# Second block's mixer: the value projection ahead of the SSM outputs, the attention outputs ahead of the gate, w_out from the attention half on

## The chip, the cores and the metric

The program runs on one core of a Trainium2 chip, in one launch. The metric is the device time of one execution in microseconds (us), taken as the median of several executions. Beside it stands one profiled execution, whose trace gives every instruction of every engine: TensorE (PE: matmuls; PEld: its weight loads), VectorE (DVE), ScalarE (ACT), GpSimd (POOL) and SyncE (SP, which here only issues DMAs).

## The reference

A sequence of 256 tokens of width 1024 goes through four transformer layers (attention of three kinds, each followed by a SwiGLU feed-forward net), all in 32-bit floats. Then comes one hybrid layer, "the second block". Its mixer, cut to what matters:

```
h = rmsnorm(x) ; u, q, k, v = split(h @ w_in)            # four parts of 512 columns
y_ssm  = gelu(C * scan(A, B u) + d * u)                  # state-space branch (SSM), from u
y_ssm  = y_ssm * sigmoid(y_ssm @ w_glu + b_glu)          # its gate
y_attn = softmax(causal(q k^T / 8)) v                    # 8 heads of 64, all 256 keys
mix = concat(rmsnorm(y_ssm) * g_ssm_out, rmsnorm(y_attn) * g_attn_out)
x = x + rmsnorm(mix @ w_out) * g_post_mix                # then a SwiGLU net closes the layer
```

The two branches meet only in `mix`: rows 0 to 511 of `w_out` multiply the SSM branch, rows 512 to 1023 the attention branch.

## The kernel before

The 256 tokens are two tiles of 128 (t = 0, 1). A weight matrix is streamed in units of 512 KB (two blocks of 128 rows by 512 columns, or one shape of the same size). `wload` (lines 155 to 159) fetches a unit into `raw` through SyncE's queue, ScalarE rounds it to `hi` (L158) and VectorE takes the rest as `lo` (L159); `mm3` (L178, L179, L180) then makes three products of 512 columns for each block of 128 rows: one unit costs 6 products for each token tile. There are 4 buffers for `raw` and 6 each for `hi` and `lo`. `proj` runs such a projection and hands the finished sums, which lie in PSUM, to a consumer; `outacc` adds a piece of an output projection into four PSUM banks.

PSUM has 8 banks: four named `acc`, two `E`, two `T`. Scratch tiles come from `work`, whose buffers are shared by size: tiles of more than 512 floats a partition have three buffers in all, those of 257 to 512 floats eight. In the mixer the large kind holds, among others, `ut` (the turned SSM input), two `xp` (the SSM states), `vs` (the values), `yo` and `ys` (the SSM outputs before and after their way back to token order).

The order of the program text is not the order in which an engine works: a planner gives each engine a fixed order ahead of the run, from its own estimate of when each instruction can go. Among those that can go it takes the one that stands first in the text. So what stands later in the text fills gaps that the planner sees. Each engine then runs its order strictly, and waits where something is late.

`mixer2` (from line 1128 on) has in its text:

1. the projection of u, the turning of u by small DMAs, the inflow products (L1174) and the scan on VectorE, which leaves `xp`;
2. the projections of q and k (after each one a fetch of a table pair `kd`, `vd` for the SSM outputs: L1124, L1125), turned by `to_T`;
3. the scores (L1225) for each t and each parity e of the head, and for each group the softmax numerators: masked maximum on VectorE (L541, L544), exponentials on ScalarE (L546), transposes (`transp`, L280) and a copy to `aTs` (L528, L530);
4. the SSM outputs: for each half b, 32 products with `ut` and 64 with `xp` (all at L252, the line of the helper `Chain`), in one `acc` bank; then the GELU (L1253 to L1259) into `yo`, and eight DMAs (L1262) that carry `yo` into `ys`;
5. the projection of v, 4 units and 48 products, in two `acc` banks, which `consu` (L1139) copies to `vs`;
6. the turning of `ys` to `yT` (L280, L272, L273) and the gate's projection with `w_glu`, in the two `E` banks, with its consumer `consg`; the gated result goes through `normed` (L1274 to L1277), which turns it into blocks 0 to 3 of `mT`;
7. the attention outputs: 16 products for t = 0 and 32 for t = 1 (L252 again, with `aTs` and `vs`), scaled, and through `normed` into blocks 4 to 7 of `mT`;
8. `w_out` rows 0 to 511 (SSM), then rows 512 to 1023 (attention), the last with the consumer that closes the layer's first part.

`normed` leaves its four transposes in a list; `pump`, called after each unit's products, takes one such entry off the list. The tail of the text that the change touches:

```
        proj(yT, [(I["w_glu_2"][0], 0, 512)], consg, tmaj=True, tags=("EE",))
        for t in range(NT):
            po, pm = psum("TE"[t]), Chain()
            ...
            normed(ya, 1.0, rows[0], t, slice(4, 8))
        outacc(acc, mT, 0, wo, 0, 4, True, False)
        ...
        outacc(acc, mT, 4, wo, 4, 4, False, True, consume)
```

Of the kernel before, what the change touches and what calls it, by code (L numbers as in the profile page):

```python
# [9 lines left out]
F32R = mybir.dt.float32r  # L10
AF = mybir.ActivationFunctionType
ALU = mybir.AluOpType
AX = mybir.AxisListType

S = 256
D = 1024
NT = 2
# [49 lines left out]
def tile_kernel(ctx, tc, I, out, upto=99):  # L67
    nc = tc.nc
    V, A, T, G = nc.vector, nc.scalar, nc.tensor, nc.gpsimd
    ids = [0]  # L70

    def nm(s):
        ids[0] += 1
        return f"{s}_{ids[0]}"
# [13 lines left out]
    def psum(tag):  # L88
        return pp.tile([128, 512], F32, tag=tag, name=nm("ps" + tag), bufs=BANKS[tag])

    def big(shape, dt=F32):
        return bp.tile(shape, dt, tag="big", name=nm("big"))

    def work(shape, tag, dt=F32):
        n = int(np.prod(shape[1:]))
        tg, b = ("w05", 4) if n <= 128 else ("w1", 3) if n <= 256 else ("w2", 8) if n <= 512 else ("w4", 3)
        if tag == "aT":
            tg = "aT"
        return wk.tile(shape, dt, tag=tg, name=nm(tag), bufs=b)
# [5 lines left out]
    def cs(t):  # L105
        return slice(t * 128, (t + 1) * 128)
# [40 lines left out]
    def row(ap, width):  # L147
        g = work([128, width], "gb")
        nc.sync.dma_start(g, ap.partition_broadcast(128))
        return g  # L150
# [13 lines left out]
    def pump(n=1):  # L164

        for _ in range(min(n, len(waiting))):
            waiting.pop(0)()
# [14 lines left out]
    def proj(xT, specs, consume, tmaj=False, kx=0, tags=(), mid=None):  # L182

        def units(spec):
            w, c0, n = spec
            nk = w.shape[0] // 128
            ku = 1024 // n if n <= 256 else 2
            for k in range(0, nk, ku):
                m = min(ku, nk - k)
                yield k, m, nk, w[k * 128:(k + m) * 128, c0:c0 + n], n  # L190

        if tmaj and len(specs) > 1 and sum(sp_[2] for sp_ in specs) > 512:
            proj(xT, specs[:1], consume, True, kx, tags[:1], mid)
            proj(xT, specs[1:], lambda i, t, p_: consume(i + 1, t, p_), False, kx, tags[1:])
        elif tmaj:
            us = []
            for sp_ in specs:
                us.append([])
                for k, m, nk, ap, n in units(sp_):
                    us[-1].append((k, nk, n, wload(ap, m, n)))  # L200
                    if mid and k == 0:
                        mid()
            for t in range(NT):
                for i, u in enumerate(us):
                    p_ = psum(tags[i][t] if i < len(tags) else "acc")
                    for k, nk, n, un in u:
                        mm3(p_[:, :n], xT, t, kx + k, un, n, k == 0, k + un[0].shape[1] == nk)
                        pump()
                    consume(i, t, p_[:, :n])
        else:  # L210
            for i, sp_ in enumerate(specs):
                p_ = [psum(tags[i][t] if i < len(tags) else "acc") for t in range(NT)]
                for k, m, nk, ap, n in units(sp_):
                    un = wload(ap, m, n)
                    for t in range(NT):
                        mm3(p_[t][:, :n], xT, t, kx + k, un, n, k == 0, k + m == nk)
                    pump()
                for t in range(NT):
                    consume(i, t, p_[t][:, :n])
# [38 lines left out]
    def newacc():  # L258
        return [[None, None] for _ in range(NT)]
# [6 lines left out]
    def split_out(dst, blocks, t, pt, scale=None):  # L266

        n = blocks.stop - blocks.start
        src = pt[:, :n * 128].rearrange("p (c q) -> p c q", c=n)
        hi, lo = dst[0][:, blocks, cs(t)], dst[1][:, blocks, cs(t)]  # L270
        if scale is None:
            A.activation(hi, src, AF.Copy)  # L272
            V.tensor_tensor(lo, src, hi.bitcast(F32), op=ALU.subtract)  # L273
        else:
            A.activation(hi, src, AF.Copy, scale=scale)
            V.scalar_tensor_tensor(lo, src, scale, hi.bitcast(F32), op0=ALU.mult, op1=ALU.subtract)

    def transp(pt, i, src):
        n = src.shape[1]
        T.transpose(pt[:n, i * 128:(i + 1) * 128], src, ident)  # L280
# [6 lines left out]
    def pair():  # L287
        return big([128, KC, S], F32R), big([128, KC, S], F32R)
# [839 lines left out]
    def mixer2(P, close):  # L1128
        hT, r = P.hT, P.r
        wt, (e_, i_, d_) = TAB["in"]  # L1130
        w = I["w_in_2"][0]
# [3 lines left out]
        tt = lambda o, a, b, op: V.tensor_tensor(o, a, b, op=op)  # L1135

        def consu(c, t, p_):
            if c == 3:
                A.activation(vs[:, t], p_, AF.Copy, scale=r[:, t:t + 1])  # L1139
                return  # L1140
            dst = work([128, 512], "qs")
            A.activation(dst, p_, AF.Copy, scale=r[:, t:t + 1])
            if c == 0:

                for q_ in range(4):
                    (G if q_ == 3 else nc.sync).dma_start(uc[32 * q_ + 16 * t:32 * q_ + 16 * t + 16], dst[:, cs(q_)])
            else:
                to_T(qkT, 4 * (c - 1), dst, 4, t, (A, V)[c - 1])
# [68 lines left out]
        for t in range(NT):  # L1217
            k = 128 * (t + 1)
            s8 = sums[t] = small(16, "s8")
            for e in range(2):  # L1220
                for pr in prs[t]:
# [5 lines left out]
                    p_ = work([128, n, k], "p2")  # L1227
                    st = small(4, "st")
                    heads(E, n, k, 0.125, st[:, 0:n], s8[:, 4 * e + pr[0]:4 * e + pr[0] + n], p_, caus[:, t, 0:k])
                    aTs[t, e, pr] = tr4([p_[:, a, cs(c)] for a in range(n) for c in range(t + 1)], (A, V)[e])  # L1230

        yb = [psum("acc"), psum("acc")]
        yo = work([128, 8, 8, 16], "yo")
        ys = work([128, NT, 512], "ys")
# [26 lines left out]
            for q_ in range(4):  # L1261
                nc.sync.dma_start(ys[:, t, cs(q_)], yo[32 * q_ + 16 * t:32 * q_ + 16 * t + 16].rearrange("c i g h -> c i (g h)"))  # L1262

        proj(hT, [(w, 1536, 512)], lambda c, t, p_: consu(3, t, p_))

        mT = pair()
        rows = [row(I[n_][0], 512) for n_ in ("g_attn_out_2", "b_glu_2", "g_ssm_out_2")]
        G.tensor_scalar(rows[2], rows[2], 0.5, None, op0=ALU.mult)

        def normed(src, half, grow, t, blocks):  # L1270

            st = small(2, "stn")
            j = work([128, 512], "junk")
            A.activation(j, src, AF.Square, scale=half * 512 ** -0.5, accum_out=st[:, 0:1])  # L1274
            rsq(st[:, 1:2], st[:, 0:1])
            o = work([128, 512], "nrm")
            V.scalar_tensor_tensor(o, src, st[:, 1:2], grow, op0=ALU.mult, op1=ALU.mult)  # L1277

            def turn():
                pt = psum("T")  # L1280
                for c in range(4):
                    transp(pt, c, o[:, cs(c)])
                split_out(mT, blocks, t, pt)

            waiting.append(turn)


        yT = (big([128, 4, S], F32R), big([128, 4, S], F32R))
        for t in range(NT):
            pt = psum("T")  # L1290
            for c in range(4):
                transp(pt, c, ys[:, t, cs(c)])
            split_out(yT, slice(0, 4), t, pt)

        def consg(c, t, p_):
            z = work([128, 512], "zg")
            tt(z, p_, rows[1], ALU.add)
            A.activation(z, z, AF.Tanh, scale=0.5)
            V.scalar_tensor_tensor(ys[:, t], z, 1.0, ys[:, t], op0=ALU.add, op1=ALU.mult)
            normed(ys[:, t], 0.5, rows[2], t, slice(0, 4))  # L1300

        proj(yT, [(I["w_glu_2"][0], 0, 512)], consg, tmaj=True, tags=("EE",))
        for t in range(NT):
            po, pm = psum("TE"[t]), Chain()
            s8 = sums[t]
            for e in range(2):
                for pr in prs[t]:
                    for a, d in enumerate(pr):
                        h = 2 * d + e
                        for c in range(t + 1):  # L1310
                            pm(po[:, 64 * h:64 * h + 64], aTs[t, e, pr][:, (t + 1) * a + c], vs[:, c, 64 * h:64 * h + 64],
                               start=(c == 0), stop=(c == t))
            pump()
            V.reciprocal(s8[:, 8:16], s8[:, 0:8])
            ya = work([128, 512], "ya")
            d4 = lambda z: z.rearrange("p (d e v) -> p d e v", d=4, e=2)
            for e in range(2):
                V.tensor_tensor(d4(ya)[:, :, e], d4(po)[:, :, e], s8[:, 8 + 4 * e:12 + 4 * e].unsqueeze(2).to_broadcast([128, 4, 64]),
                                op=ALU.mult)
            normed(ya, 1.0, rows[0], t, slice(4, 8))  # L1320
        wo = I["w_out_2"][0]
        acc = newacc()
        outacc(acc, mT, 0, wo, 0, 4, True, False)

        drain()
        nxt, consume = close()
        outacc(acc, mT, 4, wo, 4, 4, False, True, consume)
        return nxt

    def post(gain, then):  # L1330
# [123 lines left out]
```

## Time and profile before

| | |
|---|---|
| three executions | 1774.17, 1789.77, 1791.39 us |
| median | 1789.77 us |
| the profiled execution's own time | 1797.92 us |
| its span, first to last instruction | 1796.1 us |
| mean granted TensorE clock in it | 0.984 of full |

A granted clock of 1.00 is 2.4 GHz, 0.50 is 1.2 GHz. Times in the trace are counted from the first instruction. The mixer's first u products stand near 1463 us, the last products of `w_out` near 1600 us. A row of an engine's timeline gives the start, the length, the line, the operation, output and inputs and the number of merged instructions; in brackets stands the idle time ahead of it and what ended that. Matmuls are pipelined, so the lengths of neighbours overlap: the pace of a run of them is read from their starts.

### The profile page before, as it was taken

The numbers are of one execution on the slowest core, as the hardware profiler recorded it, in microseconds if no ns is written. First come the engines' busy times: TensorE is split into PE (matmuls) and PEld (weight loads), VectorE is DVE, ScalarE is ACT, GpSimd is POOL, SyncE is SP. The second block draws the span as 40 slices with busy tenths as digits, with TensorE's granted clock in tenths as the row PEclk, the third lists the DMA queues.
The fourth block names the chain that finished last, engine by engine and source line by source line (L and its number), as shares of the span: only waits on it lengthen the run. The fifth ranks groups of instructions, "written<-read, shape, count | busy, mean of one in ns | idle before, by whom it ended". The sixth has DMA issues, their size and how long they took to land.

```text
span 1796.1 us, 24258 instructions
## 1 busy us (share of the span) xinstructions
PE 1756.4 (98%) x9008; PEld 1428.5 (80%) x9008; DVE 1099.8 (61%) x1963; ACT 924.5 (51%) x1497; POOL 76.9 (4%) x100
## 2 busy tenths in 40 slices
PE   8999999999999999999999999999999998899998
PEld 6778888878888877788878888877888886678886
DVE  6766555776554664555676655777876465475554
ACT  6655444675444465555545444564544453464443
POOL 1010000110000000000100000001000010010000
PEclk9999999999999999999999999999999998799999
DMA  7346665524666554555545566534567586446662
GB/s 258 106 125 188 187 187 176 158 89 122 195 188 188 172 137 116 155 165 165 155 115 178 178 188 191 172 124 127 189 206 239 188 250 173 121 132 201 189 186 93
DMA packets 168766, 299.56 MB, mean 167 GB/s; under 512 B 20120, under 2 KB 36464, under 8 KB 167880
## 3 DMA queue, kind: packets, MB, share of 16 engines
q1 hardware_dynamic: 164936, 293.52, 53.9%
q0 software_dynamic: 3712, 4.49, 1.0%
q8 instruction: 71, 1.16, 0.3%
q14 instruction: 47, 0.39, 0.1%
HBM read 288.20 MB, written 8.68 MB: 165 GB/s over the span
## 4 chain that ended last, share of the span: by engine, by line
PE 89%; DVE 4%; DMA 3%; ACT 2%; issue 1%; POOL 1%; SPq 0%; POOLq 0%; DVEq 0%; ACTq 0%
PE psacc L179 13%; PE psacc L180 13%; PE psacc L178 13%; PE psE L178 6%; PE psE L180 6%; PE psE L179 6%; PE psT L178 6%; PE psT L179 6%; PE psT L180 6%; PE psT L280 5%; PE psT L252 3%; PE psE L739 2%; PE psE L280 1%; DVE lo L159 1%; DMA big<-kd 1%
## 5 line engine op out<-in xcount | busy, mean ns | idle before, releaser
L159 DVE TENSOR_TENSOR lo<-raw,hi 128x1024 fp32r<-128x1024 f32 (+1 forms) x528 | 637.9, 1211 | 474.3 <-ACT hi L158 473.0
L158 ACT ACTIVATE hi<-raw 128x1024 fp32r<-128x1024 f32 (+1 forms) x528 | 553.1, 1049 | 568.9 <-PE psacc L180 241.6
L178 PE MATMUL psacc<-hi,big 128*128 128x512 f32 (+1 forms) x1136 | 456.6, 402 | 1.0 <-ACT big L272 1.0
L180 PE MATMUL psacc<-hi,big 128*128 128x512 f32 (+1 forms) x1136 | 450.7, 397 | 0.0
L179 PE MATMUL psacc<-lo,big 128*128 128x512 f32 (+1 forms) x1136 | 449.3, 396 | 0.0
L180 PEld LDWEIGHTS psacc<-hi,big 128*128 128x128 f32 x1136 | 215.2, 189 | 43.5 <-issue 0.8
L178 PEld LDWEIGHTS psacc<-hi,big 128*128 128x128 f32 x1136 | 215.0, 189 | 42.9 <-issue 2.4
L179 PEld LDWEIGHTS psacc<-lo,big 128*128 128x128 f32 x1136 | 214.8, 189 | 42.2 <-issue 1.4
L178 PE MATMUL psE<-hi,big 128*128 128x512 f32 (+2 forms) x568 | 215.2, 379 | 1.4 <-ACT big L272 1.4
L179 PE MATMUL psE<-lo,big 128*128 128x512 f32 (+2 forms) x568 | 213.6, 376 | 0.0
L180 PE MATMUL psE<-hi,big 128*128 128x512 f32 (+2 forms) x568 | 213.3, 376 | 0.2 <-DVE big L273 0.2
L178 PE MATMUL psT<-hi,big 128*128 128x512 f32 (+1 forms) x480 | 178.4, 372 | 0.0
L180 PE MATMUL psT<-hi,big 128*128 128x512 f32 (+1 forms) x480 | 178.3, 372 | 0.0
L179 PE MATMUL psT<-lo,big 128*128 128x512 f32 (+1 forms) x480 | 178.3, 371 | 0.0
L178 PEld LDWEIGHTS psE<-hi,big 128*128 128x128 f32 x568 | 107.6, 189 | 22.0 <-ACT big L272 2.6
L180 PEld LDWEIGHTS psE<-hi,big 128*128 128x128 f32 x568 | 107.5, 189 | 18.8 <-DVE big L273 0.6
L179 PEld LDWEIGHTS psE<-lo,big 128*128 128x128 f32 x568 | 107.6, 189 | 18.1 <-DVE lo L159 0.2
L178 PEld LDWEIGHTS psT<-hi,big 128*128 128x128 f32 x480 | 90.4, 188 | 15.8 <-issue 0.2
L180 PEld LDWEIGHTS psT<-hi,big 128*128 128x128 f32 x480 | 90.4, 188 | 15.7
L179 PEld LDWEIGHTS psT<-lo,big 128*128 128x128 f32 x480 | 90.4, 188 | 15.6
L546 ACT ACTIVATE p<-sm,st 128x128 f32<-128x128 f32 (+2 forms) x112 | 45.9, 413 | 20.7 <-DVE st L544 20.7
L546 ACT ACTIVATE p<-psE,st 128x256 f32<-128x256 f32 x96 | 44.5, 471 | 22.0 <-DVE st L544 20.8
(292 smaller groups left out, 1635.1 us busy)
## 6 DMA issues: line engine op xcount, KB each, us to landing
raw<-in_f_w_gu SPq DMA_DIRECT2D x176, 512.0 KB, 4.1
raw<-in_f_w_out SPq DMA_DIRECT2D x88, 512.0 KB, 3.6
raw<-in_c_w_qkv SPq DMA_DIRECT2D x72, 512.0 KB, 4.1
raw<-in_a_w_qkv SPq DMA_DIRECT2D x48, 512.0 KB, 3.9
raw<-in_w_gate SPq DMA_DIRECT2D x22, 512.0 KB, 3.8
raw<-in_w_up SPq DMA_DIRECT2D x22, 512.0 KB, 3.7
raw<-in_w_down SPq DMA_DIRECT2D x22, 512.0 KB, 3.5
raw<-in_a_w_o SPq DMA_DIRECT2D x16, 512.0 KB, 4.0
```

The lines of the kernel that those rows point to most:

```text
L158: A.activation(hi, raw, AF.Copy)
L159: V.tensor_tensor(lo, raw, hi.bitcast(F32), op=ALU.subtract)
L178: T.matmul(o, a, hi[:, c, :n], start=(first and c == 0), stop=False)
L179: T.matmul(o, a, lo[:, c, :n], start=False, stop=False)
L180: T.matmul(o, b, hi[:, c, :n], start=False, stop=(last and c == nk - 1))
L252: ins = T.matmul(*a, **kw)
L280: T.transpose(pt[:n, i * 128:(i + 1) * 128], src, ident)
L546: A.activation(p[:, a], src[:, a], AF.Exp, bias=nmx[:, a:a + 1], scale=scale, accum_out=so[:, a:a + 1])
L739: T.matmul(E[:, k * a:k * a + k], qkT[64 * e:64 * e + 64, d, cs(t)], qkT[64 * e:64 * e + 64, 4 + d, k0:k0 + k], start=True, stop=True)
```

## The change

Three pieces of `mixer2`'s text move; no instruction is added, taken away or altered in its shape. The projection of v goes from behind the SSM outputs to ahead of them (behind the numerators). The attention outputs go from behind the gate to ahead of the turning of `ys`. `w_out` is taken with its attention rows first, and the SSM rows now close the sum.

```
                     aTs[t, e, pr] = tr4([p_[:, a, cs(c)] for a in range(n) for c in range(t + 1)], (A, V)[e])
 
+        proj(hT, [(w, 1536, 512)], lambda c, t, p_: consu(3, t, p_))
+
         yb = [psum("acc"), psum("acc")]
...
-        proj(hT, [(w, 1536, 512)], lambda c, t, p_: consu(3, t, p_))
-
         mT = pair()
...
-        yT = (big([128, 4, S], F32R), big([128, 4, S], F32R))
-        for t in range(NT):
-            pt = psum("T")
-            for c in range(4):
-                transp(pt, c, ys[:, t, cs(c)])
-            split_out(yT, slice(0, 4), t, pt)
-
-        def consg(c, t, p_):
...
-        proj(yT, [(I["w_glu_2"][0], 0, 512)], consg, tmaj=True, tags=("EE",))
         for t in range(NT):
             po, pm = psum("TE"[t]), Chain()
...
             normed(ya, 1.0, rows[0], t, slice(4, 8))
+
+        yT = (big([128, 4, S], F32R), big([128, 4, S], F32R))
+        for t in range(NT):
...
+        proj(yT, [(I["w_glu_2"][0], 0, 512)], consg, tmaj=True, tags=("EE",))
         wo = I["w_out_2"][0]
         acc = newacc()
-        outacc(acc, mT, 0, wo, 0, 4, True, False)
+        outacc(acc, mT, 4, wo, 4, 4, True, False)
 
         drain()
         nxt, consume = close()
-        outacc(acc, mT, 4, wo, 4, 4, False, True, consume)
+        outacc(acc, mT, 0, wo, 0, 4, False, True, consume)
```

## Rows read from the trace of the kernel before

**Rows 1.** The profile's page: span, busy time and share of TensorE, granted clock by slices.

```profile
span 1796.1 us, 24258 instructions
...
PE 1756.4 (98%) x9008; PEld 1428.5 (80%) x9008; DVE 1099.8 (61%) x1963; ACT 924.5 (51%) x1497; POOL 76.9 (4%) x100
...
PEclk9999999999999999999999999999999998799999
```

**Rows 2.** Chain that ended last, 1440 to 1620 us: start, length, work that ended last.

```profile
1491.56 18.47 DMA big<-kd
...
1553.85 4.55 DMA ys<-yo
```

**Rows 3.** Ten-microsecond windows: length, busy us by engine (instructions), PEclk, DMA share, GB/s.

```profile
1480.00:1490.00 10.00, 10.00 (x116) 8.03 (x114) 5.59 (x9) 2.71 (x3) 0.76 (x3) 1.00 0.79 256
...
1520.00:1530.00 10.00, 10.00 (x59) 4.63 (x59) 1.73 (x9) 4.60 (x18) 0.00 (x0) 0.50 0.00 0
```

**Rows 4.** Two-microsecond windows in which the granted clock fell or rose.

```profile
1508.00:1510.00 2.00, 0.00 (x0) 0.00 (x0) 0.00 (x0) 0.00 (x0) 0.00 (x0) 0.69 1.01 356
...
1538.00:1540.00 2.00, 2.00 (x18) 0.80 (x13) 1.50 (x5) 0.00 (x0) 0.00 (x0) 0.63 0.12 8
...
1556.00:1558.00 2.00, 0.00 (x0) 0.00 (x0) 0.00 (x0) 0.00 (x0) 0.00 (x0) 0.64 0.73 187
...
1562.00:1564.00 2.00, 2.00 (x7) 1.51 (x6) 0.69 (x1) 0.60 (x1) 0.00 (x0) 0.65 0.78 200
```

**Rows 5.** TensorE in order of time, SSM outputs to value projection: start, length, work, [idle].

```profile
1510.07 0.65 PE L252 MATMUL psacc<-big,ut 128*32 128x128 f32 x6 [3.63 <-DMA big<-kd]
...
1523.27 0.65 PE L252 MATMUL psacc<-big,xp 64*32 64x128 f32 x8
...
1539.99 1.30 PE L252 MATMUL psacc<-big,xp 64*32 64x128 f32 x40
1541.22 0.50 PE L178 MATMUL psacc<-hi,big 128*128 128x512 f32 x1
...
1553.15 0.39 PE L180 MATMUL psacc<-hi,big 128*128 128x512 f32 x1
```

**Rows 6.** TensorE in order of time, gate projection to first half of w_out.

```profile
1558.54 1.30 PE L280 MATMUL psT<-con,ys 128*128 128x128 f32 x5 [5.00 <-DMA ys<-yo]
...
1567.64 3.68 PE L252 MATMUL psE<-vs,aT 128*128 128x64 f32 x32
...
1571.60 1.90 PE L252 MATMUL psT<-vs,aT 128*128 128x64 f32 x16
...
1577.54 0.50 PE L178 MATMUL psacc<-hi,big 128*128 128x512 f32 x1 [0.69 <-ACT big L272]
```

**Rows 7.** The DMA queue of SyncE in order of time.

```profile
1482.25 9.22 SPq L155 DMA_DIRECT2D raw<-in_w_in  x6
1491.56 0.67 SPq L1124 DMA_DIRECT2D big<-kd  x1
```

**Rows 8.** VectorE in order of time.

```profile
1501.05 3.49 DVE L159 TENSOR_TENSOR lo<-raw,hi 128x1024 fp32r<-128x1024 f32 x3
...
1553.09 0.69 DVE L1259 SCALAR_TENSOR_TENSOR yo<-ga,yh 128x512 f32<-128x512 f32 x1
```

**Rows 9.** ScalarE in order of time.

```profile
1544.51 0.57 ACT L1253 ACTIVATE yh<-psacc 128x512 f32<-128x512 f32 x1
...
1550.85 1.07 ACT L158 ACTIVATE hi<-raw 128x1024 fp32r<-128x1024 f32 x1 [1.66 <-PE psacc L180]
...
1554.54 1.25 ACT L1139 ACTIVATE vs<-psacc,r 128x512 f32<-128x512 f32 x2
```

**Rows 10.** Groups by line, 1400 to 1620 us: work, count, busy us, mean ns, idle.

```profile
L1225 PE MATMUL psE<-big 64*128 64x128 f32 (+1 forms) x32 | 11.7, 559 | 0.0
...
L280 PE MATMUL psT<-con,p 128*128 128x128 f32 x24 | 7.7, 387 | 0.0
...
L546 ACT ACTIVATE p<-sm,st 128x128 f32<-128x128 f32 (+1 forms) x16 | 7.1, 444 | 1.9 <-DVE st L544 1.8
```

More of the change, by code (lines that the diff above doesn't have):

```diff
@@ L1285, in normed @@
             waiting.append(turn)
-        yT = (big([128, 4, S], F32R), big([128, 4, S], F32R))
-        for t in range(NT):
-            pt = psum("T")
-            for c in range(4):
-                transp(pt, c, ys[:, t, cs(c)])
-            split_out(yT, slice(0, 4), t, pt)
-        def consg(c, t, p_):
[L1296 to L1300, printed above, removed]
-        proj(yT, [(I["w_glu_2"][0], 0, 512)], consg, tmaj=True, tags=("EE",))
         for t in range(NT):
@@ L1320, in mixer2, with consg @@
             normed(ya, 1.0, rows[0], t, slice(4, 8))
+        yT = (big([128, 4, S], F32R), big([128, 4, S], F32R))
+        for t in range(NT):
+            pt = psum("T")
+            for c in range(4):
+                transp(pt, c, ys[:, t, cs(c)])
+            split_out(yT, slice(0, 4), t, pt)
+        def consg(c, t, p_):
+            z = work([128, 512], "zg")
+            tt(z, p_, rows[1], ALU.add)
+            A.activation(z, z, AF.Tanh, scale=0.5)
+            V.scalar_tensor_tensor(ys[:, t], z, 1.0, ys[:, t], op0=ALU.add, op1=ALU.mult)
+            normed(ys[:, t], 0.5, rows[2], t, slice(0, 4))
+        proj(yT, [(I["w_glu_2"][0], 0, 512)], consg, tmaj=True, tags=("EE",))
         wo = I["w_out_2"][0]
         acc = newacc()
-        outacc(acc, mT, 0, wo, 0, 4, True, False)
+        outacc(acc, mT, 4, wo, 4, 4, True, False)
         drain()
         nxt, consume = close()
-        outacc(acc, mT, 4, wo, 4, 4, False, True, consume)
+        outacc(acc, mT, 0, wo, 0, 4, False, True, consume)
         return nxt
```

## The prediction, made before the result was known

> **What bounds the kernel now.** I read the page first. TensorE is busy for 98% of the span [rows 1], so a change of order can win only two things: its idle time, and time in which its clock is halved. The slices show where the second lies: the granted clock is high everywhere but in two neighbouring slices of 45 us, 33 and 34 counted from 0, about 1482 to 1572 us, which is this mixer [rows 1]. The chain of waits for that stretch names two transfers: 18.47 us for the second table `kd`, and 4.55 us for the way of `yo` into `ys` [rows 2]. TensorE's timeline says what they cost: it stands still for 3.63 us ahead of the SSM outputs [rows 5] and for 5.00 us ahead of the turning of `ys` [rows 6]. The windows give the clock. It fell in the window of 1508 to 1510, while TensorE stood still; the mean of 0.69 puts the step at 1508.76. It rose in that of 1538 to 1540 (0.63: at 1539.48) [rows 4]. Between them TensorE worked on SSM outputs, scores and transposes without a gap and still at 0.50 (10.00 of 10 us busy from 1520 to 1530 [rows 3]). The same falling and rising goes with the second pause, from 1556.56 to 1563.40 [rows 4].
>
> What the halves cost is in the rows too: eight SSM products took 0.65 us at 0.50, 81 ns each, and forty took 1.30 us at 1.00, 33 ns each [rows 5]. From 1510.07 to 1539.48 there are 29.4 us of work at half clock; at full clock they are 14.7 us.
>
> **The parts, one by one.**
>
> *Value projection earlier.* Its 48 products of 512 columns are unchanged: first at 1541.22, last at 1553.15 [rows 5], 12.3 us with the transposes between them, 48 x 0.227 = 10.9 us alone. Are its weights there earlier? Yes: all its four fetches are out by 1491.5, ahead of the second `kd` in SyncE's queue [rows 7], and VectorE ends their last `lo` at 1504.54 [rows 8]. So they can begin where the k projection ends, about 1505.5; now they lie ready for 37 us. Text order says that they take the planner's gaps ahead of the SSM outputs. The pause of 3.63 us for `kd` is then covered by 10.9 us of products: **-3.6 us** (bounds 0 and -3.63). SyncE's queue keeps its order: the four fetches are past the tables already.
>
> *The clock.* With that pause gone, and 512-column products between the scores and the transposes, I let the clock stay high: **-14.7 us**. The bounds are far apart: 0 if the small products run at 0.50 again, -14.7 if none does. I take the far end because of two rows: the clock fell while TensorE stood still [rows 4], and 116 mostly small products in 10 us left it at 1.00 as long as no pause came [rows 3]. That busy small products do not bring it back is also in these rows, and is what a rival below rests on. The Trainium skill ("TensorE: Matmul & The Clock Gate", "What's actually happening") says that "the default state is throttled, and activity releases the throttle". The trace agrees with its first half only: activity of the kind in this stretch did not release it for 29 us. By that rule steady work of any kind would hold the clock up in the changed kernel, which gives the sum below; by the rows it may not, which is the first rival.
>
> *Softmax, no longer hidden.* Its engines had twice the time so far. Now, from 1505.5 to the SSM outputs, TensorE has 10.9 us of values, half of the scores' 11.7 us and half of the transposes' 7.7 us [rows 10], together 20.6 us; ScalarE's exponentials take 7.1 us [rows 10] in a chain with VectorE's maxima. TensorE remains the longer one. I add **+1.3 us**, an estimate: three of the exponentials' 0.44 us that nothing covers; the bounds are 0 and the whole 7.1 us.
>
> *A new wait.* `vs` is a large scratch tile, and three buffers serve that kind. `ut` and both `xp` hold them until the last SSM product, at 1541.3 in the old run [rows 5]. So the copy of the values (1.25 us for two [rows 9]) cannot run ahead of that end, however early the products are; until then the sums lie in two `acc` banks, which nobody else wants yet, the SSM halves having the other two. Behind these copies in ScalarE's order stand the GELU of the last half and the `hi` of `w_out`; the attention outputs wait for them, so TensorE stands still about 0.7 us (bounds 0 and 1.25).
>
> *Attention outputs earlier.* 48 products, 3.68 + 1.90 us [rows 6], unchanged. They no longer cover the gate's tail, but the way from the last SSM product to `ys`. That way is now 17.3 us (1541.3 to 1558.54), and 12.3 us of values cover it. How long will it be? Of the 17.3 us the first GELU step starts at 1544.51, behind the exponentials, and a `hi` in the middle waits 1.66 us for TensorE to free a buffer [rows 9]. From the end of `yo`, 1553.78 [rows 8], to the first transpose are 4.8 us. Six GELU steps of about 0.6 us add 3.6: the least is 8.3 us, the most 17.3. I take 10, near the least, since exponentials and value products are over by then, and two copies stand in the way. Cover: 0.7 + 5.6 = 6.3 us, so 3.7 us remain, with the 0.7 us above 4.4 instead of 5.0: **-0.6 us** (bounds -2.3 and +6.7). The clock may fall there as before; I count no difference.
>
> *w_out from its attention half on.* 96 products either way, eight fetches either way, only which half first; the fetches wait for `raw` buffers as before. 48 products, 10.9 us, now cover the gate's tail, which the attention outputs and one unit did not quite cover: the wait of 0.69 us [rows 6] goes, **-0.7 us** (bounds -0.7 and +1.0, the second if the attention half's own transposes come late). GpSimd's small powers only change places.
>
> Sum: -3.6 - 14.7 + 1.3 - 0.6 - 0.7 = **-18.3 us**. The profiled execution took 1797.92 us, 1.8 more than its span; with the sum it would take 1779.6. It stands 8.15 us above the median of 1789.77; that median less 18.3 is 1771.5. I say **1772**, 1.0% less. One of the three executions took 1774.17, some 16 us less than the others; I read it, without its trace, as one in which the clock did not fall. It would gain only about 4 us, so the median of new runs of the old kernel matters too.
>
> **The rivals.**
>
> *The clock falls again in part (1783).* For: busy small products at 0.50 did not bring it back [rows 3]. If the value products are used up early and any pause follows, the 192 SSM products run late and slow: 192 x (81 - 33 ns) = 9.2 us are given back, up to the whole 14.7 us with the scores. That makes 1781 to 1786; I take 1783. Against: those products stand in one run without a transfer to wait for.
>
> *Slower (1793).* Place: TensorE, between the last SSM product and `ys`. If ScalarE and VectorE still need 17.3 us there, because `hi` of `w_out` or the `vs` copies stand ahead of the GELU, 5.6 us of attention outputs cover less than the values did: 11.7 us of idle for 5.0, +6.7. Should the clock also gain nothing, 6.7 - 3.6 = +3.1 us: 1793. It decides when the way stays over 14.2 us (10.6 would break even with 5.0, and 3.6 more with the gain at `kd`) and the small products stay at 0.50. For: six `hi` buffers, four of them freed early, let more weight work in. Against: both waits that lengthened the way have left.
>
> *It does not do what it says (1789).* The planner might leave the values behind the SSM outputs. Against: it let SSM products into every gap of the scores because they were next in the text.
>
> **Chances.** Forecast 0.55, its own range 1764 to 1779; clock in part 0.26; slower 0.11; no effect 0.08. One per cent, about what a measurement of this kernel can tell from no change, is 17.9 us: 1771.9 and 1807.7. The forecast lies on that edge: two thirds of it, with the weight of a shorter way to `ys`, count as faster (0.36) and a little of the second case (0.02). Slower by over 1% needs 18 us more, well beyond the third case's price: 0.07, the part of it in which the `vs` copies or a `hi` hold ScalarE far longer. Same: 0.55. Range for 8 in 10: 1762 to 1788, which leaves out the slow case and the far ends.
>
> **What would show it.** Right: no wait for `kd` ahead of the SSM outputs; L178 to L180 into `acc` between scores and transposes before the first L252; PEclk 1.00 from 1505 to about 1535; `vs` copied within 1 us after the last SSM product; the last SSM product near 1534, where the last value product now ends at 1553.5; a pause of 3 to 5 us ahead of the turning of `ys`. Wrong: PEclk 0.50 for more than 10 us, a pause of over 10 us ahead of `ys`, or transposes that wait for exponentials by more than 5 us in all.

## The result, and the profile after

| | before | after |
|---|---|---|
| median of 8 runs each | 1783.01 us (1772.68 to 1793.55) | 1767.17 us (1761.68 to 1768.53) |
| ratio, 95% interval | | 0.989 [0.986, 0.992] |
| the profiled execution, its span | 1797.92, 1796.1 us | 1766.45, 1764.7 us |
| mean granted TensorE clock in it | 0.984 | 0.998 |

The change makes the kernel 1.1% faster: 1772 was predicted, with 1762 to 1788 as the range. The likeliest case came about and its sum came near, but two of its terms were mis-sized in opposite directions and a third was not seen at all.

The page of the changed kernel: span, busy time, granted clock by slices.

```profile
span 1764.7 us, 24253 instructions
...
PE 1734.2 (98%) x9008; PEld 1418.4 (80%) x9008; DVE 1099.9 (62%) x1963; ACT 925.0 (52%) x1497; POOL 73.0 (4%) x100
...
PEclk9999999999999999999999999999999999999999
```

The two slices of low clock [rows 1] are gone. The number of matmuls is the same (x9008), and TensorE is busy for 22 us less: most of what was won is not idle time, but work that takes less time.

Five-microsecond windows of the changed kernel (length, busy us by engine, PEclk, DMA share, GB/s), where before had stretches at 0.50 [rows 3] and windows of 0.63 to 0.69 in which the clock fell or rose [rows 4]:

```profile
1505.00:1510.00 5.00, 5.00 (x23) 3.22 (x22) 3.38 (x25) 3.87 (x14) 0.00 (x0) 1.00 0.48 180
...
1520.00:1525.00 5.00, 5.00 (x98) 4.03 (x100) 4.86 (x6) 2.77 (x6) 0.00 (x0) 1.00 0.66 217
...
1535.00:1540.00 5.00, 4.47 (x24) 3.06 (x23) 2.36 (x5) 1.80 (x4) 0.57 (x1) 1.00 0.68 150
```

TensorE's timeline of the changed kernel, from the last turning of k to the end of `w_out`'s first token tile:

```profile
1500.67 0.60 PE L280 MATMUL psT<-con,qs 128*128 128x128 f32 x4
...
1503.36 1.71 PE L1225 MATMUL psE<-big 64*128 64x128 f32 x16
1505.00 0.50 PE L179 MATMUL psacc<-lo,big 128*128 128x512 f32 x1
...
1522.61 1.08 PE L252 MATMUL psacc<-big,ut 128*32 128x128 f32 x32
1523.62 1.95 PE L252 MATMUL psacc<-big,xp 64*32 64x128 f32 x64
1525.51 1.08 PE L252 MATMUL psacc<-big,ut 128*32 128x128 f32 x32
1526.52 1.95 PE L252 MATMUL psacc<-big,xp 64*32 64x128 f32 x64
1528.40 2.00 PE L252 MATMUL psT<-vs,aT 128*128 128x64 f32 x16
1530.23 3.74 PE L252 MATMUL psE<-vs,aT 128*128 128x64 f32 x32
1534.64 0.63 PE L280 MATMUL psT<-con,nrm 128*128 128x128 f32 x4 [0.67 <-DVE nrm L1277]
1535.12 0.30 PE L280 MATMUL psT<-con,ys 128*128 128x128 f32 x1
1535.95 0.50 PE L178 MATMUL psacc<-hi,big 128*128 128x512 f32 x1 [0.53 <-ACT big L272]
...
1547.75 0.63 PE L280 MATMUL psT<-con,nrm 128*128 128x128 f32 x4 [0.59 <-DVE nrm L1277]
...
1554.29 0.63 PE L280 MATMUL psT<-con,nrm 128*128 128x128 f32 x4 [0.22 <-DVE nrm L1277]
...
1564.80 1.32 PE L280 MATMUL psacc<-con,x 128*128 128x128 f32 x8 [0.32 <-DVE x L1346]
```

The values' products (L178 to L180) stand between scores and transposes, and the 192 SSM products, which before lay in pieces of 2 to 40 between them [rows 5], follow in one run of 5.8 us with no wait ahead. The attention outputs follow without idle time. The 5.00 us ahead of the turning of `ys` [rows 6] are gone: the transposes of `ys` start at 1535.12 with no wait of their own. The 0.67 us just ahead of them are a wait for `nrm`, the normed attention outputs of the first token tile. Between single transposes of `ys` stand products of `w_out`'s attention half.

ScalarE, VectorE and SyncE's queue around the way from the SSM outputs to `ys`, in the changed kernel:

```profile
1525.64 0.60 ACT L1255 ACTIVATE yh<-psacc 128x512 f32<-128x512 f32 x1 [1.86 <-PE psacc L252]
...
1526.81 1.25 ACT L1139 ACTIVATE vs<-psacc,r 128x512 f32<-128x512 f32 x2
...
1531.78 0.69 DVE L1261 SCALAR_TENSOR_TENSOR yo<-ga,yh 128x512 f32<-128x512 f32 x1
...
1500.47 24.96 SPq L155 DMA_DIRECT2D raw<-in_w_out  x8
...
1532.56 5.14 SPq L1264 DMA_DIRECT2D ys<-yo  x8
...
DMA to landing us min/median/max: 2.4/2.4/2.4
```

The same last line for before's `ys` reads:

```profile
DMA to landing us min/median/max: 4.0/4.3/4.5
```

The values are copied at 1526.81, while the last 64 SSM products are still running. All eight fetches of `w_out` are out by 1525.43; in before, six of the eight go out from 1534.05 on, three of them right ahead of the `ys` transfers. In the changed kernel, with nothing of `w_out` ahead of them, these land after 2.4 us instead of 4.3. The experiments below fall the same way: medians of 2.4 or 2.5 us where nothing stood ahead (1, 3, 5, 7), 3.1 to 4.2 us behind three fetches (2, 4, 6, 8).

**The ledger.** I take the stretch from the mixer's first product of u to the eight transposes of `x` that follow `w_out`'s first token tile: 1463.35 to 1596.23 before, 1459.72 to 1564.80 after, 132.88 and 105.08 us. It holds 27.8 of the 31.4 us by which the two spans differ; the other 3.6 lie ahead of it, where nothing was changed. Part of these is the clock too: earlier in the program it stands at 0.50 for some 17 us of before's profile (in the windows 710 to 715, 755 to 765, 800 to 810 and 850 to 870) and for some 7 us of the changed kernel's (755 to 765).

| in that stretch | predicted | measured |
|---|---|---|
| pause for `kd` | -3.6 | -3.63 |
| clock, 1508.76 to 1539.48 | -14.7 | -12.7 |
| softmax uncovered | +1.3 | 0 |
| SSM products in one run | not seen | -3.2 (what is left over) |
| from the last value or SSM product to the end | -1.3 | -6.45 |
| a wait of q's transposes for ScalarE, 1.78 us, in before's profile only | | -1.78 |

How the measured ones come out: in before, the work between the pause and the first value product took 31.15 us (1510.07 to 1541.22). Experiment 2 below has the same pieces in the same order, and from its first eight `xp` products on it has them at 1.00: 16.75 us (1506.20 to 1522.95) for 28.10 in before, from this line to 1541.22:

```profile
1513.12 0.65 PE L252 MATMUL psacc<-big,xp 64*32 64x128 f32 x8
```

The three pieces ahead of that line come to 1.71 us, an estimate from pieces of their kind at 1.00 in experiments 2 and 4 (0.34, 0.58 and 0.79 us from start to next start): 31.15 - 16.75 - 1.71 = 12.7. The end runs from 1553.38 to 1596.23 before (the last value product starts at 1553.15 and takes 0.23 us at its neighbours' pace), 42.85 us, and from 1528.40 to 1564.80 after, 36.40 us, with the same products in both. The wait of 1.78 us is in none of the experiments 2, 4, 6 and 8, which leave the order there as it was, so I count it to the run and not to the change.

### The profile page after: what moved, and what is told of

The parts are those of the page before. It is cut to its first block, busy times and chain, and to the rows that moved or that the text cites. A ratio compares the mean times of both kernels' runs of the same rounds, so it can differ in the third digit from the quotient of the medians.

```text
span 1764.7 us, 24253 instructions
## 1 busy us (share of the span) xinstructions
PE 1734.2 (98%) x9008; PEld 1418.4 (80%) x9008; DVE 1099.9 (62%) x1963; ACT 925.0 (52%) x1497; POOL 73.0 (4%) x100
## 4 chain that ended last, share of the span: by engine, by line
PE 89%; DVE 4%; ACT 2%; issue 1%; POOL 1%; DMA 1%; SPq 0%; DVEq 0%; POOLq 0%; ACTq 0%
PE psacc L179 13%; PE psacc L180 13%; PE psacc L178 13%; PE psE L178 7%; PE psE L180 7%; PE psE L179 7%; PE psT L178 6%; PE psT L180 6%; PE psT L179 6%; PE psT L280 4%; PE psT L252 3%; PE psE L739 2%; DVE lo L159 1%; PE psE L280 1%; PE psacc L280 1%
## 5 line engine op out<-in xcount | busy, mean ns | idle before, releaser
L178 PE MATMUL psacc<-hi,big 128*128 128x512 f32 (+1 forms) x1136 | 455.8, 401 | 0.9 <-ACT big L272 0.9
L180 PE MATMUL psacc<-hi,big 128*128 128x512 f32 (+1 forms) x1136 | 449.5, 396 | 0.0
L180 PEld LDWEIGHTS psacc<-hi,big 128*128 128x128 f32 x1136 | 214.3, 189 | 43.2 <-issue 0.6
L178 PEld LDWEIGHTS psacc<-hi,big 128*128 128x128 f32 x1136 | 214.2, 189 | 42.2 <-issue 2.0
L178 PE MATMUL psE<-hi,big 128*128 128x512 f32 (+2 forms) x568 | 215.1, 379 | 1.2 <-ACT big L272 1.2
L180 PE MATMUL psE<-hi,big 128*128 128x512 f32 (+2 forms) x568 | 213.5, 376 | 0.2 <-DVE big L273 0.2
L178 PE MATMUL psT<-hi,big 128*128 128x512 f32 (+1 forms) x480 | 178.5, 372 | 0.0
L180 PE MATMUL psT<-hi,big 128*128 128x512 f32 (+1 forms) x480 | 178.4, 372 | 0.0
L178 PEld LDWEIGHTS psE<-hi,big 128*128 128x128 f32 x568 | 107.6, 189 | 21.2 <-ACT big L272 1.9
L180 PEld LDWEIGHTS psE<-hi,big 128*128 128x128 f32 x568 | 107.4, 189 | 19.2 <-DVE big L273 0.8
L178 PEld LDWEIGHTS psT<-hi,big 128*128 128x128 f32 x480 | 90.4, 188 | 15.7 <-issue 0.2
L180 PEld LDWEIGHTS psT<-hi,big 128*128 128x128 f32 x480 | 90.5, 188 | 15.7
```

Of the source, the lines that this page charges most:

```text
L178: T.matmul(o, a, hi[:, c, :n], start=(first and c == 0), stop=False)
L180: T.matmul(o, b, hi[:, c, :n], start=False, stop=(last and c == nk - 1))
```

## The experiments

All are whole programs, timed beside the kernel before: the first four on one chip (31 runs of before, median 1785.04), the next three on another (17 runs, 1781.9), the last on a third (15 runs, 1782.68). Before's 63 runs fall into two groups with nothing between: 40 with a mean granted clock of 0.991 to 0.996, median 1780.4 us, and 23 with 0.984 to 0.988, median 1794.3 us. The profiled run of before (0.984) is of the second group, and this is needed to read every ratio below. The medians of the group of high clock are 1779.8, 1780.6 and 1782.1 us on the three chips, so times from different chips can be some 2 us apart for that reason alone.

**1. The value projection alone.** `e1`: the kernel before with only that line moved.

```diff
+        proj(hT, [(w, 1536, 512)], lambda c, t, p_: consu(3, t, p_))
+
         yb = [psum("acc"), psum("acc")]
...
-        proj(hT, [(w, 1536, 512)], lambda c, t, p_: consu(3, t, p_))
```

> The value projection alone is moved ahead of the SSM outputs; attention outputs and w_out stand as in the kernel before. Theory (the pause for kd and the clock that fell in it were most of the loss): no pause ahead of the SSM outputs, PEclk 1.00 there, -18 us against a run of before whose clock falls. But nothing stands between the last SSM product and the turning of ys: a pause of 6 to 7 us there (the way from the last SSM product to ys took 6.7 us in the changed kernel), after which the clock falls for some us. Time 1773 to 1776, ratio about 0.994. Rival (the gain is mainly that the attention outputs cover the way to ys): 1780 or more.

Measured: 1776.63 us, ratio 0.995 [0.992, 0.998]; the clock of its ten runs 0.991 to 0.995. The wait for `kd` is gone and the clock stays at 1.00 up to the end of the SSM outputs. Then nothing covers the way to `ys` (TensorE's timeline, then a window):

```profile
1526.83 1.95 PE L252 MATMUL psacc<-big,xp 64*32 64x128 f32 x64
1535.43 0.45 PE L280 MATMUL psT<-con,ys 128*128 128x128 f32 x1 [6.65 <-DMA ys<-yo]
```

```profile
1535.00:1540.00 5.00, 3.86 (x10) 2.01 (x11) 0.69 (x1) 0.60 (x1) 0.00 (x0) 0.50 0.55 89
```

The planner left the attention outputs behind the gate, where the text has them. Why it did not put them into this gap no run shows; the text gives the two `T` banks and the two `E` banks, of which they need one each, to the turning of `ys` and to the gate first. So the first part alone wins what stands ahead of the SSM outputs and makes the second pause longer: 6.65 us and a halved clock behind it, for 5.00 before [rows 6].

**2. The tail alone.** `e2`: the changed kernel with the value projection back behind the SSM outputs.

```diff
-        proj(hT, [(w, 1536, 512)], lambda c, t, p_: consu(3, t, p_))
-
         yb = [psum("acc"), psum("acc")]
...
+        proj(hT, [(w, 1536, 512)], lambda c, t, p_: consu(3, t, p_))
+
         mT = pair()
```

> The value projection stays behind the SSM outputs; attention outputs ahead of the gate and w_out from its attention half on, as in the change. Theory: the pause for kd (3.6 us) and the half clock after it stay; the second pause (5.0 us, ahead of the turning of ys) is covered by the 5.6 us of attention outputs and the clock does not fall there: -5 to -7 us, ratio about 0.996, a clock trace with PEclk 0.50 from the pause on to about 1540 us and 1.00 after. Rival (the tail's new order is worth nothing by itself): ratio 0.999 to 1.002.

Measured: 1781.3 us, ratio 0.997 [0.994, 1.001]: inconclusive against no effect. Three of its ten runs have a clock of 0.985 or 0.986 and take 1790.28 to 1796.26; the median of the other seven is 1776.31. TensorE's timeline and windows of the profiled run:

```profile
1503.14 0.65 PE L252 MATMUL psacc<-big,ut 128*32 128x128 f32 x6 [2.50 <-DMA big<-kd]
...
1506.20 0.42 PE L252 MATMUL psacc<-big,xp 64*32 64x128 f32 x8
...
1522.95 0.50 PE L178 MATMUL psacc<-hi,big 128*128 128x512 f32 x1
...
1536.99 2.00 PE L252 MATMUL psT<-vs,aT 128*128 128x64 f32 x16 [1.72 <-ACT vs L1139]
```

```profile
1500.00:1505.00 5.00, 2.50 (x24) 1.33 (x26) 1.34 (x3) 0.59 (x1) 0.00 (x0) 0.78 0.99 292
1505.00:1510.00 5.00, 5.00 (x62) 3.57 (x54) 2.45 (x18) 0.71 (x1) 0.00 (x0) 0.88 0.50 186
```

Here the pause for `kd` is back (2.50 us), the clock falls (the 0.78 puts that at 1502.8) and is at 1.00 again from about 1506.2 (the 0.88), with the same small products that in before's profile ran at 0.50 to 1539. So both profiled runs have the pause, and only one of them the long half clock. And a new wait shows: the attention outputs stand 1.72 us for the copy of the values, since the values' products now end right ahead of them.

**3. `w_out` from its SSM half on.** `e3`: the changed kernel with the two halves in before's order. A `drain()`, which takes the turning of all finished blocks, has to come ahead of the first half, since that half now reads the last block turned.

```diff
         acc = newacc()
-        outacc(acc, mT, 4, wo, 4, 4, True, False)
+        drain()
+        outacc(acc, mT, 0, wo, 0, 4, True, False)
 
         drain()
         nxt, consume = close()
-        outacc(acc, mT, 0, wo, 0, 4, False, True, consume)
+        outacc(acc, mT, 4, wo, 4, 4, False, True, consume)
```

> The changed kernel with w_out taken from its SSM half on, as before; since the text then asks for the last turned block before w_out, the list of waiting transposes is emptied ahead of it. Theory (order of w_out's halves is worth the 0.7 us of one wait plus what its products fill among the transposes of ys): the attention half's products can no longer fill the gaps of the ys transposes, and the gate's tail of some 7 to 10 us stands bare in part: 3 to 8 us more than the changed kernel, 1770 to 1775. Rival: under 1 us more.

Measured: 1775.61 us, ratio 0.994 [0.991, 0.997]; 8.4 us above the changed kernel's 1767.17. TensorE's timeline and one window:

```profile
1532.96 0.33 PE L280 MATMUL psT<-con,ys 128*128 128x128 f32 x1 [0.28 <-DMA ys<-yo]
...
1546.11 1.09 PE L280 MATMUL psT<-con,nrm 128*128 128x128 f32 x4 [2.62 <-DVE nrm L1277]
1547.88 0.79 PE L178 MATMUL psacc<-hi,big 128*128 128x512 f32 x1 [0.69 <-ACT big L272]
```

```profile
1545.00:1550.00 5.00, 3.21 (x9) 2.41 (x10) 3.79 (x6) 1.84 (x4) 0.18 (x1) 0.60 0.56 170
```

The order of the halves, which I priced at 0.7 us, is worth up to 8.4. The SSM half can't begin before the gate's tail has been normed and turned, so nothing fills TensorE between the single transposes of `ys` (0.28 us and three like it) or behind the gate (2.62 + 0.69 us), and the clock falls (0.60 in this window). How much of that is the `drain()`'s own is not separated.

**4. Before without the wait for the second table.** `e4`: the kernel before, but both halves of the SSM outputs read the first table pair. The second is fetched and not read: this kernel, as those of 6 to 8, leaves out the second half's own tables. The products are before's, in nearly before's order: the planner cuts the SSM outputs into somewhat other pieces (at the head 10, 22, 10 and 14 for 4, 6, 22, 8, 2 and 10).

```diff
-        tt_, vt = zip(*got)
+        tt_, vt = zip(got[0], got[0])
```

> The kernel before, in which the SSM outputs read the first table pair for both halves of the states; the second pair is still fetched and not read, so no product waits for it. Order on every engine as before. Theory (a pause lets the clock fall, and small products alone leave it up): no pause of 3.6 us, PEclk 1.00 through scores and SSM outputs, the value projection ends some 18 us earlier; ratio about 0.990 to 0.993 with the second pause still there. Rival (only the 512-column value products among them hold the clock up): PEclk 0.50 there all the same, only 3.6 us gained, ratio 0.998.

Measured: 1776.94 us, ratio 0.996 [0.993, 0.999]; the clock of its ten runs 0.992 to 0.996, none lower. A window and the second pause:

```profile
1520.00:1525.00 5.00, 5.00 (x88) 3.09 (x87) 3.54 (x11) 3.59 (x10) 0.00 (x0) 1.00 0.33 108
```

```profile
1541.46 1.98 PE L280 MATMUL psT<-con,ys 128*128 128x128 f32 x5 [4.09 <-DMA ys<-yo]
```

The same small products run at 1.00, from 1505 to 1540, once the pause ahead of them is gone. In this stretch it was the pause that let the clock fall, not the kind of products. The value products were not needed for the clock as such; they were needed to fill the pause. A pause is not the only thing behind which the clock falls, though. Earlier in before's profile it falls at about 710, with TensorE busy without a gap from 700.4 on; ahead of it pairs of scores alternate with lone transposes (a window, the last pair, a window):

```profile
706.00:708.00 2.00, 2.00 (x12) 1.25 (x10) 1.57 (x15) 1.80 (x10) 0.00 (x0) 1.00 0.12 46
```

```profile
709.54 0.48 PE L739 MATMUL psE<-big 64*128 64x128 f32 x2
```

```profile
711.00:712.00 1.00, 1.00 (x5) 0.68 (x3) 0.00 (x0) 1.00 (x7) 0.00 (x0) 0.50 0.00 0
```

Against the 17 runs of before beside it that have the high clock (median 1779.82) this kernel gains 2.9 us, about the pause; against all 31 it gains 8.1.

**5. The changed kernel again**, on the second chip, unchanged.

> The changed kernel itself, beside the others of this call. Theory (every execution keeps the clock, so the long times of the kernel before are gone): all clocks 0.996 or more, 1765 to 1769 us in every run, ratio 0.989.

Measured: 1766.04 us, ratio 0.988 [0.984, 0.992]. With the eight runs above, all 14 have a clock of 0.996 to 0.999 and a median of 1766.9.

**6. The tail, without the wait for the second table.** `e6`: `e2` with the edit of 4.

```diff
-        tt_, vt = zip(*got)
+        tt_, vt = zip(got[0], got[0])
```

> Tail as in the change, value projection behind the SSM outputs as before, and the SSM outputs read the first table pair for both halves of the states, so that nothing waits for the second. Theory (the values' move is worth the pause for kd and the clock that falls in it, and nothing else): within 3 us of the changed kernel, 1767 to 1771, no run under a clock of 0.99. Rival (the 512-column products among scores and SSM outputs are needed too): 1775 or more, clocks under 0.99 in some runs.

Measured: 1777.19 us, ratio 0.995 [0.992, 0.998]. My expectation that this would come to the changed kernel's time fell. TensorE's timeline and windows:

```profile
1537.45 2.92 PE L252 MATMUL psT<-vs,aT 128*128 128x64 f32 x16 [1.72 <-ACT vs L1139]
1540.17 7.04 PE L252 MATMUL psE<-vs,aT 128*128 128x64 f32 x32
```

```profile
1535.00:1540.00 5.00, 3.28 (x20) 2.82 (x18) 2.20 (x3) 2.21 (x3) 0.00 (x0) 0.83 0.76 248
...
1550.00:1555.00 5.00, 5.00 (x23) 4.17 (x22) 2.42 (x4) 1.20 (x2) 0.11 (x1) 0.80 0.66 238
```

There is no `kd` pause, but the wait of 1.72 us for the values is there, and behind it the clock is halved from about 1538.3 to 1552.0 (from the 0.83 and the 0.80), 13.7 us of work. From the first attention output on, the same products up to the start of the gate's third took 14.7 us here (1537.45 to 1552.17) and 8.9 in experiment 2 (1536.99 to 1545.84): 5.9 us lost. So the early value projection has a third use beside the pause and the clock: the values are copied long before the attention outputs want them.

**7. The changed kernel without the wait for the second table.** The edit of 4 on the changed kernel.

```diff
-        tt_, vt = zip(*got)
+        tt_, vt = zip(got[0], got[0])
```

> The changed kernel in which the SSM outputs read the first table pair for both halves of the states. Theory (the values cover the fetch of the second pair whole): the same time as the changed kernel within 1.5 us. Rival (part of the wait is left): 2 us less or more.

Measured: 1764.42 us, ratio 0.988 [0.984, 0.992], 1.6 us below 5, with ranges that overlap (1762.55 to 1766.87; 1761.19 to 1767.19). Neither trace has a wait for `kd`: the changed kernel has nothing left to win there.

**8. As 6, without the wait for the values.** `e8`: the attention outputs multiply `ut` in place of `vs`, a tile that is there early; so their results are not attention's.

```diff
-  pm(..., vs[:, c, 64 * h:64 * h + 64],
+  pm(..., ut.rearrange("p (t g) c -> p t (g c)", t=2)[:, c, 64 * h:64 * h + 64],
```

> As the last but one (tail as in the change, values behind the SSM outputs, second table pair not read), but the attention outputs multiply with the turned SSM input, a tile of the same shape that is ready long before, in place of the values, so that they need not wait for the copy of the values. Theory (the 11 us that this order still lacks against the changed kernel are that wait of 1.7 us and the half clock of some 14 us, 6.9 us lost, that comes with it): no pause there, PEclk 1.00 on the attention outputs, 1767 to 1770 us, ratio 0.990. Rival (the copy is not it, and the values must stand among scores and SSM outputs): 1775 or more, ratio 0.995.

Measured: 1770.64 us, ratio 0.993 [0.990, 0.995]: 6.6 of the 11.2 us between 6 and 5 are back, and the clock stays at 1.00 there. (The wait and the half clock were 1.7 + 5.9 us; the chip is another.) What is left stands in TensorE's timeline:

```profile
1507.55 0.41 PE L252 MATMUL psacc<-big,xp 64*32 64x128 f32 x4
1507.89 0.33 PE L280 MATMUL psT<-con,p 128*128 128x128 f32 x1
1508.15 0.42 PE L252 MATMUL psacc<-big,xp 64*32 64x128 f32 x6
...
1509.36 0.42 PE L252 MATMUL psacc<-big,xp 64*32 64x128 f32 x8
1509.71 0.33 PE L280 MATMUL psT<-con,p 128*128 128x128 f32 x1
1509.97 0.42 PE L252 MATMUL psacc<-big,xp 64*32 64x128 f32 x6
...
1531.17 1.89 PE L252 MATMUL psT<-ut,aT 128*128 128x64 f32 x16
```

Four, six and eight SSM products between two lone transposes all take the same 0.34 to 0.35 us from start to next start, and each lone transpose 0.26. In one run of 192 they take 30 ns each (5.79 us in the changed kernel), so eight would be 0.24 and four 0.12. The longer pieces of this run go up in steps: 0.55 to 0.57 us for 10 and 14 products, 0.77 and 0.78 for 18 and 22, 1.23 for 40; the changed kernel's pieces of 32 and 64 take 1.01 and 1.88. All of these are within 0.02 us of 0.12 us for the piece and 0.22 for each eight begun. So a cut costs twice, by one more 0.12 and by eights that are not full.

TensorE is busy in both kernels without idle time and at 1.00 from the first of k's last eight transposes to the attention outputs, over the same products: 1499.41 to 1531.17 here, 31.8 us, and 1500.67 to 1528.40 in the changed kernel, 27.7 us. The 4.0 us between them are the price of the alternation: some 2.9 in the SSM pieces (8.7 for 5.8 us) and the rest in the transposes. They are near the 3.2 us left over in the ledger, which is reckoned from before's own pieces.

The Trainium skill ("TensorEngine Tiling (Array Packing)", "Key Properties") says that a change of tiling mode drains TensorE. The trace agrees in so far as products on 64 rows by 32 columns that alternate with transposes on 128 by 128 cost more at each change; that a drain is what takes the time, no run separates. Products of 512 columns, which have the transposes' shape, lie better beside them: a pair of transposes adds 0.22 us among them (changed kernel, at 1515.42) and 0.36 between SSM pieces (here, at 1516.72).

## Why the prediction was right, and where it was not

**The forecast case was the right one.** No wait for `kd`; value products between scores and transposes; the clock at 1.00 throughout; TensorE gapless up to the last SSM product, 27.7 us after k's end where I had 28.5 (1505.5 to 1534). The first rival, the clock falling again in part, didn't come: by their mean clocks in none of 14 runs. Its ground was that busy small products at 0.50 did not bring the clock back. That holds for before's profiled run; in experiment 2 the same products were at 1.00 again from 1506.2 on, and in experiment 4 they kept the clock up. That they keep it up is no rule elsewhere (the fall at 710, under experiment 4). The Trainium skill's rule that the prediction weighed ("TensorE: Matmul & The Clock Gate", "What's actually happening"), that activity releases the throttle, agrees with experiment 2's trace and, for 29 us, not with before's. The "slower" rival needed a way of over 14.2 us to `ys`; it is 6.7. And the change did what it says.

**The clock term, mis-sized twice.** In the profiled run it was 12.7 us and not 14.7. I halved all 29.4 us, but the same products in the same order took 26.4 us at 0.50 (1513.12 to 1539.48) and 15.0 at 1.00 (experiment 2's 16.75 less the last 1.74, which ran at 1.00 in before too), a ratio of 1.76 and not 2. And I took the sum, made against the profiled run of before, off the median. Only 23 of before's 63 runs have the low clock; the groups lie 13.9 us apart, of the size of the term. The prediction saw the sign of it, the run of 1774.17, but said that such a run "would gain only about 4 us". It gains 13.5 (1780.4 to 1766.9), by the terms that follow. That before's runs of high clock are runs in which the clock came back soon after the pause is argued from experiments 2 and 4; none of them was profiled. The size fits: before's profile has 30.7 us at 0.50 here and experiment 2's 3.4; 27 us more at half clock in a span of 1796 lower the mean by 0.008, as far as the groups stand apart (0.994 and 0.986).

**The way to `ys`, the step that failed.** I took 10 us for it and a pause of 4.4 us, "The clock may fall there as before; I count no difference". It is 6.7 us (1528.40 to 1535.12), below my least of 8.3. That bound carried over the 4.8 us from `yo`'s end to the first transpose, which here are 2.65: I took the transfers' landing as fixed, while the queue ahead of them was to empty. There is no wait for `ys`, the clock doesn't fall, and idle time in the end part is 2.0 us (0.67 + 0.53 + 0.59 + 0.22) for 6.5 (5.00 + 0.47 + 0.69 + 0.20 + 0.15). That is -4.5, and the half clock from 1556.56 to 1563.40 [rows 4] went with it, some 4.4 us of work, -2.2: together -6.7, for the 6.45 of the ledger. The term for `w_out`'s order, -0.7, belongs here too. Besides covering the gate's tail, its attention half fills TensorE between the transposes of `ys` as they land one by one, which I didn't see; experiment 3 prices it at up to 8.4 us.

**Not seen: the SSM products in one run**, -3.2 to -4.0 us. The rows had it: eight products took 0.65 us in pieces, forty 1.30 [rows 5], and I put the whole difference down to the clock. At 1.00 eight in a piece still take 0.35 us to the next start, 44 ns each.

**The wait for `vs` did not occur.** "`ut` and both `xp` hold them until the last SSM product" was wrong in its first word: in each half the products with `ut` come ahead of those with `xp`, so `ut`'s buffer is free two microseconds before the last SSM product, and the copy ran there. Experiments 2 and 6 show what the wait costs where it is met: 1.72 us, and in 6 the clock. **Softmax** cost 0 for +1.3: no transpose waited for an exponential.

**The sum.** Against the profiled run 18.3 us were predicted; by the ledger the change gave 3.63 + 12.7 + 3.2 + 6.45 = 26.0, and the rest of the 31.5 us lies in the runs. Against before's median, 15.8 us measured, 18.3 came near by luck, by two errors that offset each other: the clock term too large for most runs, the end and the SSM run too small. The 1772 also started from a median of three runs, 1789.77; that of eight is 1783.01. The parts do not add up, either. Against before's runs of high clock the value projection alone gives 3.2 us (1779.82 to 1776.63), the tail alone, in its seven runs of high clock, 3.5 (to 1776.31), the two together 13.5. Each removes one pause and alone leaves, or makes, another, with half clock behind it in its profiled run.

## What to carry to other kernels

Where the granted clock falls behind a wait, compare the mean clock of all runs before subtracting its cost from a median: a profiled run can belong to the smaller group. Price small matmuls by the piece they stand in, not each by itself (here 0.12 us for the piece and 0.22 for each eight begun), and let them run in one block with full-width products among the transposes. And when a chain of transfers sits behind a pause, ask both what else is in that queue and which products can start without its end; taking the half of a sum that is ready first cost nothing here and was worth up to 8 us.

## What the runs showed of the hardware that I had not expected

- The same pause can have two outcomes. The wait of 1.72 us for the values was followed by 13.7 us at 0.50 in experiment 6 and left the clock at 1.00 in the profiled run of experiment 2. Behind the `kd` pause the clock was back in the next ten microseconds in experiment 2 (2.50 us of pause) and stayed at 0.50 for 29 us of gapless work in before (3.63 us). What decides between them is open; in experiments 4 and 8, without the pause in question, the clock did not fall there.
- The clock can fall with TensorE busy without a gap: earlier in before's profile at about 710, behind pairs of scores that alternate with lone transposes.
- Half the clock is not twice the time where shapes alternate: 26.4 us for 15.0.
- Small products cost by the piece, in steps of eight: at 1.00, 2 to 8 took 0.34 to 0.36 us, 10 and 14 took 0.55 to 0.57, 64 took 1.88.
- A 64 KB transfer of `ys` landed after 2.4 us with SyncE's queue clear, and after 4.3 us behind three fetches of 512 KB; in the experiments 2.4 or 2.5 and 3.1 to 4.2.
